# One decoder block on one core: channel-pair steps behind the weight splits at the passage to gate/up, and down's weight loads behind their splits

## The chip, the cores and the metric

The kernel runs on one core of one Trainium2 chip, as one launch. The metric is the device time of an execution in microseconds. The time before is the median of three runs. The profile is of one further execution, whose own time is given beside its span (first to last instruction).

## What is computed

One layer on 512 tokens of 2048 channels, in float32: an RMS norm, a joint input projection into three token mixers (dilated attention, convolution, sliding-window attention), an output projection with a residual, and a SwiGLU feed-forward part with 5632 hidden columns and a second residual. The change lies in the second half:

```python
def reference(x, ...):
    ...
        x = x + mix @ w_out[l]
        h2 = _rms_norm(x, norm2_g[l])
        x = x + (jax.nn.silu(h2 @ w_gate[l]) * (h2 @ w_up[l])) @ w_down[l]
    return x
```

## The kernel before

**Matrix products in three parts.** Every float32 product is made of three matmuls on rounded halves: high weight times high activation, low weight times high, high weight times low. A weight tile of 128 x 1024 is therefore split before use into `wh` (high) and `wl` (low). For gate/up and down a split is three operations: ScalarE (ACT) copies the raw weights, reordered, into `wn` in PSUM (L268) and into `wh` in SBUF (L269), and VectorE (DVE) subtracts to get `wl` (L270). There are three buffers of `wh` and `wl` and two of `wn`.

**Products of blocks.** Gate/up and down multiply 2 x 2 blocks with seven products in place of eight (Strassen's scheme in Winograd's form). Each of seven products needs a block or a sum of blocks of the weights and of the activations. The weight sums (`s`, `21`, `11`, made of the raw blocks `11`, `12`, `21`, `22`) are made by GpSimd (POOL) in place, at L172. `ORDER` and `D_ORDER` give the order of the products. Gate/up runs 11 blocks (`Up`) of 2 x 7 products of two units each, so 28 units of 12 matmuls per block (L1184, L1186, L1187); `u0`, `u1`, ... name the weights of half a block, `A` and `B` the two units of a product. Down runs 12 blocks of 14 units (`Down`, L1431 to L1433), with weights `d0` to `d11`; an A unit has 12 matmuls, a B unit 12 or 6.

**One list of weight units.** `works` holds every unit of the kernel in order: input projection, output projection, gate/up, down. Those of gate/up and down are marked `"moves"`. `next_unit()` hands out the next one, and beside that does three things ahead: `sums_now()` issues POOL's sums that are due at this unit, `split_up_to(u + SPLIT_AHEAD)` issues the splits up to two units ahead, and `pump(limit, most)` issues loads of raw weights (L242) on SyncE's (SP's) queue, as long as the next load's buffer is free and fewer than `limit` tiles are held, at most `most` of them. A buffer becomes free, in the program's order, when the last split that reads it is issued. Engines run their own instructions in the order in which the program issues them; SP's queue is one such order, with the loads of weights, of activations (`a<-od`, L1318), and the stores.

**Steps by ticks.** Work between projections is spread over the matmuls by a clock of its own, `Ticks`: `ticks.after(n, fn)` files a step, `ticks.tick()` runs what is due, `ticks.drain()` runs all. After each channel tile of the output projection is done, five steps follow at one tick each: `residual` (L984), `scale_x2` (store x2, scale it by the norm's weights, L992 and L994), `differences` (block differences of two channel tiles, L1014 to L1022; channel pair j is tiles j and j + 8), `high` (ACT casts, L1028) and `low` (DVE subtractions, L1034). Beside them the squares of x2 are added up into `ssum2` (L1004, and the addition that is recorded at L97). What `high` and `low` make, `ops[q, j]`, are gate/up's activations; pairs 0 to 3 are read by a block's first seven products, pairs 4 to 7 by the second seven. The projection ends with the tiles 6, 7, 14 and 15, that is with pairs 6 and 7.

**The passage.** Between the projection's last matmul and gate/up's first, the kernel before runs two ticks, issues the splits up to two units ahead, runs three more ticks and then drains all that is left.

**`norm2()`** turns `ssum2` into the norm's factor: eight small matmuls into `r2s` (L349), in one of the two PSUM buffers that `wn` uses, a DVE operation (L421) and a POOL operation (L422). It is called after gate/up's fourth unit. The factor is first used at the second seven products.

**Loads in down.** In `next_unit()` the units marked `"moves"` load before they split: at most two loads, and only into buffers that an earlier unit's split had freed. After the unit's matmuls, `load_next` issues one or two activation reads (two in the first block).

Of the kernel before, what the change touches and what calls it, by code (L numbers as in the profile page):

```python
# [52 lines left out]
RAW_BUFS = 8  # L53
RAW_EARLY = 5
SPLIT_BUFS = 3
X_AHEAD = 8
SPLIT_AHEAD = 2
# [59 lines left out]
def kernel(ctx: ExitStack, tc: tile.TileContext, xT, wi, wo, wgu, wd, cst_in, outT):  # L117
# [18 lines left out]
    ticks = Ticks()  # L136
# [12 lines left out]
    entries, works = [], []  # L149
# [4 lines left out]
    def take(buf, key, n=1024):  # L154
        assert buf not in held
        held[buf] = key
        raws[key] = (wp.tile([P, 1024], F32, name=f"w{key}", tag=f"raw{buf}", bufs=1), n)
        return raws[key][0]

    def drop(key):  # L160
        for buf in [b for b, k in held.items() if k == key]:
            held.pop(buf)
        return raws.pop(key)
# [5 lines left out]
    def plus(to, a, b, n, buf=None):  # L169
        def go():  # L170
            out = take(buf, to, n) if buf else raws[to][0]
            nc.gpsimd.tensor_add(out[:, :n], raws[a][0][:, :n], raws[b][0][:, :n])  # L172
        return go

    def up_block(pair, m, half, j):

        return [bass.AP(tensor=wgu.tensor, offset=wgu.offset + (4 * (pair + i * NP) + 2 * m + half) * P * 1024 + j * P,
                        ap=[[1024, P], [4 * P * 1024, 2], [1, 2 * P]]) for i in range(2)]
# [4 lines left out]
    for n in range(2 * NBLOCKS):  # L183
        base = len(works)
        keys = {c: {k: (k, f"u{n}{c}") for k in ("11", "12", "21", "22", "s")} for c in "AB"}
        for k in ("21", "11", "22", "12"):
            for i, c in enumerate("AB"):
                entries.append((bufs[c]["s" if k == "12" else k], keys[c][k],
                                up_block(n // 2 * 2, 2 - int(k[0]), int(k[1]) - 1, n % 2 * 4 + 2 * i)))
        for i, c in enumerate("AB"):  # L190
            key = keys[c]
            sums[base - 4 + i].append(plus(key["s"], key["21"], key["11"], 1024, bufs[c]["s"]))
            sums[base + i].append(plus(key["21"], key["21"], key["22"], 1024))
            sums[base + 2 + i].append(plus(key["11"], key["21"], key["11"], 1024))
            sums[base + 7 + i].append(plus(key["11"], key["11"], key["12"], 1024))
        works.extend((keys[c][k], last, "moves") for k, last in (
            ("s", True), ("11", False), ("22", True), ("11", False), ("21", True), ("12", True), ("11", True)) for c in "AB")
        bufs = {c: {"21": b["22"], "11": b["21"], "s": b["s"], "22": b["11"]} for c, b in bufs.items()}

    def down_block(g, i, half, first, end):  # L200
# [31 lines left out]
    at = {"entry": 0, "split": 0, "use": 0}  # L232

    def pump(limit, most=99):
        while at["entry"] < len(entries) and len(raws) < limit and entries[at["entry"]][0] not in held and most:
            most -= 1
            buf, key, parts = entries[at["entry"]]
            size = [part.shape[-1] * (part.shape[1] if len(part.shape) == 3 else 1) for part in parts]
            t, o = take(buf, key, sum(size)), 0
            for part, n in zip(parts, size):  # L240
                to = t[:, o:o + n]
                nc.sync.dma_start(to.rearrange("p (n f) -> p n f", n=part.shape[1]) if len(part.shape) == 3 else to, part)  # L242
                o += n
            at["entry"] += 1


    lows, late_lows = [], []

    def lows_now():
        while lows:  # L250
            fn, *args = lows.pop(0)
            fn(*args)  # L252
        if late_lows:
            pump(RAW_EARLY if at["use"] <= 20 else RAW_BUFS)

    def split_up_to(i):
        while at["split"] <= min(i, len(works) - 1):
            key, last, eng = works[at["split"]]
            t, n = drop(key) if last else raws[key]
            u = at["split"]  # L260
            hi = wp.tile([P, 1024], F32R, name=f"wh{u}", tag="hi", bufs=SPLIT_BUFS)
            lo = wp.tile([P, 1024], F32R, name=f"wl{u}", tag="lo", bufs=SPLIT_BUFS)
            if eng == "moves":

                near = psum["high"].tile([P, 1024], F32R, name=f"wn{u}", tag="h")
                src = t[:, :n].rearrange("p (n f c) -> p f n c", n=4, c=P)
                by = lambda x: x[:, :n].rearrange("p (f n c) -> p f n c", n=4, c=P)
                nc.scalar.copy(by(near), src)  # L268
                nc.scalar.copy(by(hi), src)  # L269
                nc.vector.tensor_sub(by(lo), src, by(near).bitcast(F32))  # L270
            elif eng or "high" not in psum:
                eng = eng or nc.vector

                (nc.vector.tensor_copy if u == 0 else nc.scalar.copy)(hi[:, :n], t[:, :n])  # L274
                lows.append((eng.tensor_sub, lo[:, :n], t[:, :n], hi[:, :n].bitcast(F32)))
                if not late_lows:
                    lows_now()
            else:
                near = psum["high"].tile([P, 1024], F32R, name=f"wn{u}", tag="h")
                nc.scalar.copy(near[:, :n], t[:, :n])  # L280
                nc.scalar.copy(hi[:, :n], t[:, :n])
                lows.append((nc.vector.tensor_sub, lo[:, :n], t[:, :n], near[:, :n].bitcast(F32)))
                if not late_lows:
                    lows_now()
            splits[u] = (hi, lo)
            at["split"] += 1

    def sums_now():
        for fn in sums.pop(at["use"], ()):
            fn()  # L290

    def next_unit():
        sums_now()
        u = at["use"]
        at["use"] += 1
        moves = works[u][2] == "moves"
        if moves:
            pump(RAW_BUFS, 2)
        lows_now()
        split_up_to(u + SPLIT_AHEAD)  # L300
        if not lows and not moves:
            pump(RAW_EARLY if u < 20 else RAW_BUFS)
        return splits.pop(u)

    def mm3(out, wh, wl, xh, xl, start, stop):
# [755 lines left out]
                m_hi.pop(row), m_lo.pop(row)  # L1061
    lows_now()

    ticks.tick()
    ticks.tick()
    split_up_to(at["use"] + SPLIT_AHEAD)
    for _ in range(3):
        ticks.tick()
    lows_now()
    ticks.drain()  # L1070
    b = m_hi = m_lo = r1b = mult_a = bias_a = bias_c = over = upper = None

    lows_now()
# [8 lines left out]
    def norm2():  # L1082

        b = psum["high"].tile([P, 1024], F32, name="r2s", tag="h")[:, :NT]
        n2["r"] = token_scale(ssum2, D, "n2", b)[1]
# [19 lines left out]
    def later(n, fn, *args, queue=evacs):  # L1105
        while len(queue) <= n:
            queue.append([])
        queue[n].append((fn, *args))
# [179 lines left out]
    def turn_x2(key):  # L1288

        z = turns[key] = slot("z")  # L1290
        for part in range(4):
            nc.sync.dma_start(by_blocks(z, part), turned(x2d, key, part))
# [14 lines left out]
    def load_next(n, limit=99):  # L1307
        while feed and n and len(acts) < limit:
            key = feed.pop(0)
            n -= 1  # L1310
            if len(key) == 4:
                y[key] = slot("y")
                nc.sync.dma_start(y[key], x2t[key])
            else:
                q, j = key
                acts[key] = slot(f"a{q}_{j}", F32R)
                at = LAID.index(q)
                nc.sync.dma_start(acts[key].bitcast(F32), od[j][:, at * T:(at + 1) * T])  # L1318

    for n in range(NBLOCKS):  # L1320
        blk = Up(n)
        for blk.first in (0, 4):
            for i, q in enumerate(ORDER):
                for c, _ in enumerate(blk.product(q)):
                    at_unit = (7 if blk.first else 0) * 2 + 2 * i + c
                    if n == 0 and at_unit == 3:
                        norm2()
                    if 1 <= n <= 8 and at_unit in (9, 23):
                        key = SUMS[2 * n - 2 + at_unit // 16]
                        turn_x2(key)  # L1330
                        later(6, turn_x2_now, key)
                    if n == NBLOCKS - 1 and blk.first:
                        load_next(2)
                if n == NBLOCKS - 1:
                    for j in range(4):
                        ops.pop((q, blk.first + j))
# [24 lines left out]
    class Down:  # L1361
# [74 lines left out]
        def sum(self, i, k, a):  # L1436
            return self.g, i, k, a
# [139 lines left out]
```

## Time and profile before

| what | value |
|---|---|
| median of three runs | 1874.36 us (1873.17 to 1876.38) |
| the profiled execution | 1873.66 us, span 1871.9 us |
| mean granted TensorE clock | 0.996 |
| PE (matmuls) busy | 1849.2 us, 99% of the span |
| DVE, ACT, POOL busy | 1432.8, 1321.8, 1106.1 us |
| moved by DMA | 330.36 MB, 176 GB/s over the span |

In the profile an engine's row tells when it worked and what ended its idle time. A line of the timeline has start and duration in microseconds, engine, source line, operation, the tile written and those read, the shapes, and in brackets the idle time before it with the instruction that ended it. In the view of windows each row is a stretch: its length, the busy time of PE, of the weight loads (PEld), DVE, ACT and POOL with their counts, the granted TensorE clock (1.00 is full speed), the busy share of the 16 DMA engines and their GB/s. SPq is SyncE's queue of DMA issues.

### The profile page before, as it was taken

To read this page: it belongs to the slowest core of one execution; us is meant where nothing else is said; L and a number is where in the kernel's file an instruction comes from. 1 tells how busy PE (TensorE), PEld (TensorE's weight loads), DVE (VectorE), ACT (ScalarE), POOL (GpSimd) and SP (SyncE) were. 2 spreads that over 40 slices of the span, in tenths; PEclk is the share of its full clock that TensorE was granted. 3 is DMA by queue.
4 is the path that set the end of the run, shared out by engine and by line. 5 is a ranking of instruction groups with operands and counts; after the bars stand their busy time and mean duration, and the time that the engine had idled before them with its cause. 6 is when DMAs were issued, how large, how long until landed. Compare 5 with 4: busy or idle time off the path is not lost.

```text
span 1871.9 us, 26621 instructions
## 1 busy us (share of the span) xinstructions
PE 1849.2 (99%) x8370; PEld 1530.4 (82%) x8370; DVE 1432.8 (77%) x2052; ACT 1321.8 (71%) x1794; POOL 1106.1 (59%) x850
## 2 busy tenths in 40 slices
PE   9999999999999999999999999999999899999998
PEld 7888888888887888888888888888888677888887
DVE  6778878998688777777777777777777577777777
ACT  6355644553457788887888888888888577778775
POOL 0135533100003467786887778868777789879775
PEclk9999999999999999999999999999999999999999
DMA  7242253343333356777867776777679887566545
GB/s 272 76 146 92 78 144 97 91 130 123 131 136 96 113 152 187 199 209 180 228 176 199 222 193 190 213 189 219 177 220 303 272 263 264 202 222 230 181 134 113
DMA packets 382988, 330.36 MB, mean 176 GB/s; under 512 B 171648, under 2 KB 311552, under 8 KB 382848
## 3 DMA queue, kind: packets, MB, share of 16 engines
q1 hardware_dynamic: 382704, 328.66, 59.3%
q8 instruction: 66, 1.08, 0.2%
q14 instruction: 74, 0.61, 0.1%
q10 hardware_dynamic: 144, 0.01, 0.0%
HBM read 255.56 MB, written 64.63 MB: 171 GB/s over the span
## 4 chain that ended last, share of the span: by engine, by line
PE 93%; POOL 2%; DMA 2%; issue 1%; DVE 1%; ACT 1%; SPq 0%; POOLq 0%; ACTq 0%; DVEq 0%
PE out L1184 15%; PE out L1186 15%; PE out L1187 15%; PE out L1431 6%; PE out L1432 6%; PE out L1433 6%; PE o L306 3%; PE o L308 3%; PE o L307 3%; PE cq L306 2%; PE cq L307 2%; PE cq L308 2%; PE ak L306 1%; PE aq L306 1%; PE av L306 1%
## 5 line engine op out<-in xcount | busy, mean ns | idle before, releaser
L1184 PE MATMUL out<-wh,h 128*128 128x512 f32 x1232 | 480.5, 390 | 4.3 <-ACT wh L269 4.3
L1186 PE MATMUL out<-wl,h 128*128 128x512 f32 x1232 | 480.4, 390 | 0.0
L1187 PE MATMUL out<-wh,h 128*128 128x512 f32 x1232 | 480.2, 390 | 0.0
L1184 PEld LDWEIGHTS out<-wh,h 128*128 128x128 f32 x1232 | 231.8, 188 | 52.8 <-ACT wh L269 4.7
L1186 PEld LDWEIGHTS out<-wl,h 128*128 128x128 f32 x1232 | 231.8, 188 | 48.4 <-DVE wl L270 0.3
L1187 PEld LDWEIGHTS out<-wh,h 128*128 128x128 f32 x1232 | 231.8, 188 | 48.3
L1431 PE MATMUL out<-wh,a 128*128 128x512 f32 x620 | 242.9, 392 | 11.5 <-ACT wh L269 11.5
L1432 PE MATMUL out<-wl,a 128*128 128x512 f32 x620 | 242.3, 391 | 0.8 <-DVE wl L270 0.8
L1433 PE MATMUL out<-wh,a 128*128 128x512 f32 x620 | 241.6, 390 | 0.0
L274 ACT CAST wh<-w 128x1024 fp32r<-128x1024 f32 (+2 forms) x94 | 96.8, 1031 | 152.6 <-PE o L307 64.5
L1431 PEld LDWEIGHTS out<-wh,a 128*128 128x128 f32 x620 | 117.2, 189 | 39.3 <-ACT wh L269 15.3
L252 DVE TENSOR_TENSOR wl<-w,wh 128x1024 fp32r<-128x1024 f32 (+2 forms) x95 | 113.5, 1195 | 41.3 <-ACT wh L274 39.9
L1432 PEld LDWEIGHTS out<-wl,a 128*128 128x128 f32 x620 | 117.2, 189 | 26.6 <-DVE wl L270 2.0
L1433 PEld LDWEIGHTS out<-wh,a 128*128 128x128 f32 x620 | 117.1, 189 | 23.6
L1441 DVE TENSOR_TENSOR y<-y,out 128x512 f32<-128x512 f32 x164 | 106.1, 683 | 21.9 <-PE out L1433 20.2
L517 DVE SCALAR_TENSOR_TENSOR y<-bu,cst,y 128x511 f32<-128x511 f32 (+14 forms) x120 | 89.8, 749 | 0.7
L306 PE MATMUL o<-mh_c,wh 128*128 128x512 f32 x128 | 51.1, 399 | 0.0
L306 PE MATMUL cq<-hh,wh 128*128 128x512 f32 x128 | 50.5, 395 | 0.0
L308 PE MATMUL o<-mh_c,wl 128*128 128x512 f32 x128 | 50.0, 391 | 0.0
L307 PE MATMUL cq<-hl,wh 128*128 128x512 f32 x128 | 49.9, 390 | 0.0
L307 PE MATMUL o<-ml_c,wh 128*128 128x512 f32 x128 | 49.9, 390 | 0.0
L308 PE MATMUL cq<-hh,wl 128*128 128x512 f32 x128 | 49.9, 390 | 0.0
(2376 smaller groups left out, 4881.3 us busy)
## 6 DMA issues: line engine op xcount, KB each, us to landing
od<-a SPq DMA_DIRECT2D x154, 256.0 KB, 4.1
a<-od SPq DMA_DIRECT2D x154, 256.0 KB, 5.6
w<-in_wi SPq DMA_DIRECT2D x58, 512.0 KB, 3.3
w<-in_wo SPq DMA_DIRECT2D x32, 512.0 KB, 3.3
x<-in_xT SPq DMA_DIRECT2D x16, 256.0 KB, 7.0
xr<-in_xT SPq DMA_DIRECT2D x16, 256.0 KB, 3.6
x2d<-xr SPq DMA_DIRECT2D x16, 256.0 KB, 2.0
z<-x2d SPq DMA_DIRECT2D x64, 64.0 KB, 3.8
```

Source lines behind the costliest of these rows:

```text
L252: fn(*args)
L274: (nc.vector.tensor_copy if u == 0 else nc.scalar.copy)(hi[:, :n], t[:, :n])
L306: nc.tensor.matmul(out, wh, xh, start=start, stop=False)
L307: nc.tensor.matmul(out, wh, xl, start=False, stop=False)
L308: nc.tensor.matmul(out, wl, xh, start=False, stop=stop)
L1184: nc.tensor.matmul(b, x[:, high], wh[:, s], start=c == f == 0 and q in (7, 1, 5, 2), stop=False, skip_group_check=True)
L1186: nc.tensor.matmul(b, x[:, high], wl[:, s], start=False, stop=False, skip_group_check=True)
L1187: nc.tensor.matmul(b, x[:, low], wh[:, s], start=False, stop=c == f == 1, skip_group_check=True)
L1431: nc.tensor.matmul(b[:, lo:hi], x[:, high], wh[:, s], start=start, stop=False, skip_group_check=True)
L1432: nc.tensor.matmul(b[:, lo:hi], x[:, high], wl[:, s], start=False, stop=False, skip_group_check=True)
L1433: nc.tensor.matmul(b[:, lo:hi], x[:, low], wh[:, s], start=False, stop=last, skip_group_check=True)
L1441: getattr(eng, op)(t, t, src)
```

## The change

Three edits.

1. At the passage, one split is issued, then one tick is run, then the next split; the ticks that were run there and the drain are gone. What is left of the steps of pairs 6 and 7 runs in gate/up's loop, one tick after each unit.
2. `norm2()` is called after gate/up's 13th unit in place of the 4th.
3. In `next_unit()` only gate/up's units (those before `turned_to`) load ahead of their split. Down's units load after it, again at most two, so that the load goes out one unit earlier in the program's order and into the buffer that this split has just freed, and in SP's queue it stands ahead of the activation reads of that unit.

```diff
             ("s", True), ("11", False), ("22", True), ("11", False), ("21", True), ("12", True), ("11", True)) for c in "AB")
+        turned_to = len(works)
...
         moves = works[u][2] == "moves"
-        if moves:
+        ahead = moves and u < turned_to
+        if ahead:
             pump(RAW_BUFS, 2)
         lows_now()
         split_up_to(u + SPLIT_AHEAD)
-        if not lows and not moves:
-            pump(RAW_EARLY if u < 20 else RAW_BUFS)
+        if not lows and not ahead:
+            pump(RAW_EARLY if u < 20 else RAW_BUFS, 2 if moves else 99)
         return splits.pop(u)
...
     lows_now()
 
-    ticks.tick()
+    split_up_to(at["use"] + SPLIT_AHEAD - 1)
     ticks.tick()
     split_up_to(at["use"] + SPLIT_AHEAD)
-    for _ in range(3):
-        ticks.tick()
-    lows_now()
-    ticks.drain()
     b = m_hi = m_lo = r1b = mult_a = bias_a = bias_c = over = upper = None
...
                     at_unit = (7 if blk.first else 0) * 2 + 2 * i + c
-                    if n == 0 and at_unit == 3:
+                    if ticks.due:
+                        ticks.tick()
+                    if n == 0 and at_unit == 12:
                         norm2()
```

The order in which the instructions are built changes at the passage on ACT and DVE, at `norm2` on PE, DVE and POOL, and from down's first block on in SP's queue. No instruction is added or removed.

## The prediction

> **What bounds the kernel now.** The page first: TensorE's row against the span.
>
> ```profile
> span 1871.9 us, 26621 instructions
> PE 1849.2 (99%) x8370; PEld 1530.4 (82%) x8370; DVE 1432.8 (77%) x2052; ACT 1321.8 (71%) x1794; POOL 1106.1 (59%) x850
> ```
>
> PE (TensorE's matmuls) is busy for 99% of the span, so an edit that removes no matmul can only win PE's idle time and the stretches in which its clock is low. The waits of PE say where it idles:
>
> ```profile
> PE out L1431 <- ACT wh L269: 11.5, 8, 2.6
> PE out L1184 <- ACT wh L269: 4.3, 1, 4.3
> PE out L1432 <- DVE wl L270: 0.8, 2, 0.7
> ```
>
> One wait of 4.3 us lies at L1184 (gate/up), eight of 11.5 us together at L1431 (down), both ended by ACT's `wh` at L269, a copy of a weight split; 0.8 us more by DVE's `wl`. The windows show the rest:
>
> ```profile
> 594.68:600.15 5.47, 5.47 (x12) 4.09 (x13) 3.61 (x4) 5.47 (x7) 2.39 (x1) 0.50 0.18 57
> 650.00:1400.00 750.00, 750.00 (x3310) 621.02 (x3310) 571.90 (x652) 625.20 (x760) 571.75 (x402) 1.00 0.72 196
> 1560.00:1860.00 300.00, 300.00 (x1325) 248.43 (x1324) 225.55 (x269) 229.12 (x259) 242.42 (x141) 1.00 0.60 190
> ```
>
> From 650 to 1400 us and from 1560 to 1860 us PE is busy without a gap at clock 1.00: nothing can be won there. Between 594.68 and 600.15 the granted clock is 0.50. So two places remain, the passage from output projection to gate/up and the first blocks of down, and the change edits both.
>
> I number gate/up's first units by their weights: 1 `s` A, 2 `s` B, 3 `11` A, 4 `11` B, 5 `22` A, 6 `22` B, 7 `11` A again. Each is 12 matmuls. PE's timeline in the passage:
>
> ```profile
> 582.08 0.39 PE L1184 MATMUL out<-wh,h 128*128 128x512 f32 x1
> 590.01 0.39 PE L1187 MATMUL out<-wh,h 128*128 128x512 f32 x1
> 594.68 0.79 PE L1184 MATMUL out<-wh,h 128*128 128x512 f32 x1 [4.28 <-ACT wh L269]
> 595.30 0.80 PE L1186 MATMUL out<-wl,h 128*128 128x512 f32 x1
> 600.15 0.95 PE L349 MATMUL r2s<-ones,ssum 128*128 128x1 f32 x8
> 600.96 0.48 PE L1184 MATMUL out<-wh,h 128*128 128x512 f32 x1
> ```
>
> **The passage, before.** From 582.08 (unit 1's first matmul) to 590.01 (unit 3's last) are 35 steps, so one takes 0.227 us and a unit 2.72 us. Without a wait unit 4 would start at 590.24 and unit 5 at 592.96. Unit 5 starts at 600.96: 8.0 us later. Of these 0.8 us (600.15 to 600.96) are the eight small `r2s` matmuls of `norm2`, which the change keeps and only moves. The loss that can be won is 7.2 us: 4.4 us until 594.68, and 2.7 us because twelve matmuls took 5.47 us at clock 0.50.
>
> **Why PE waited.** The splits of units 3 and 4 stand on ACT and DVE (VectorE) behind the steps of the last two channel pairs, pair 6 and pair 7 (L1020 to L1034 on DVE, L1028 on ACT), and one of those steps is held. DVE's timeline, and in the last row POOL's:
>
> ```profile
> 582.85 0.68 DVE L984 TENSOR_TENSOR xr<-xr,o 128x512 f32<-128x512 f32 x1
> 585.45 1.22 DVE L270 TENSOR_TENSOR wl<-w('11', 'u0A')_5517,wn 128x1024 fp32r<-128x1024 f32 x1 [1.32 <-ACT wn L268]
> 586.59 0.42 DVE L1034 TENSOR_TENSOR h<-ta,h 128x256 fp32r<-128x256 f32 x1
> 586.93 2.65 DVE L1034 TENSOR_TENSOR h<-tb,h 128x256 fp32r<-128x256 f32 x1
> 590.51 0.41 DVE L1020 TENSOR_TENSOR ta<-h,h 128x256 f32<-128x256 f32 x1
> 591.75 0.68 DVE L97 TENSOR_TENSOR ssum<-ssum,sr 128x512 f32<-128x512 f32 x1
> 592.36 0.42 DVE L1034 TENSOR_TENSOR h<-ta,h 128x256 fp32r<-128x256 f32 x1
> 594.03 1.21 DVE L270 TENSOR_TENSOR wl<-w('11', 'u0B')_5572,wn 128x1024 fp32r<-128x1024 f32 x1
> 586.90 2.39 POOL L172 TENSOR_TENSOR w('11', 'u0A')_5517<-w('21', 'u0A')_5464,w('11', 'u0A')_5517 128x1024 f32<-128x1024 f32 x1 [9.79 <-DVE wl L270]
> ```
>
> Unit 3's `wl` runs at 585.45 and unit 4's only at 594.03. Between them stand two sets of five subtractions. The first takes 0.34 us to the next (586.59 to 586.93), but the second lasts 2.65 us: POOL (GpSimd) starts its sum `11` + `21` at 586.90, freed by unit 3's `wl`, and the subtraction ends when POOL does. From the set's start to the next operation (590.51) are 3.92 us, 2.24 us over five such steps. [...]
>
> **The change, part 1: the order at the passage.** As the instructions are built, ACT now has: unit 3's split, pair 6's five casts, the last x2 scaling, unit 4's split, ..., unit 5's split, pair 7's casts, unit 6's split. DVE has: last `xr` addition, unit 3's `wl`, one `ssum` addition, unit 4's `wl`, pair 6's five subtractions, three operations L1020 to L1022, a copy from PSUM (L1197), unit 5's `wl`, the last `ssum` addition, unit 6's `wl`, pair 7's five subtractions. Nothing is added or removed, and SP's queue keeps its order here, so the loads cost nothing. ACT's steps come from its timeline before:
>
> ```profile
> 581.08 0.62 ACT L1004 ACTIVATE sr<-xr 128x512 f32<-128x512 f32 x1
> 582.56 0.41 ACT L1028 CAST h<-tb 128x256 fp32r<-128x256 f32 x1
> 583.79 0.72 ACT L994 ACTIVATE h<-xr,cst 128x512 f32<-128x512 f32 x1
> 584.42 1.00 ACT L268 CAST wn<-w('11', 'u0A')_5517 128x1024 fp32r<-128x1024 f32 x1
> 585.36 1.04 ACT L269 CAST wh<-w('11', 'u0A')_5517 128x1024 fp32r<-128x1024 f32 x1
> 586.30 0.63 ACT L1004 ACTIVATE sr<-xr 128x512 f32<-128x512 f32 x1
> ```
>
> Worked forward with the same durations. ACT's `sr` of 581.08 takes 0.62, so unit 3's `wn` starts at 581.7, its `wh` at 582.6 (0.94 each to the next, 584.42 to 585.36 to 586.30). Five casts at 0.31 (582.56 to 583.79 are four) run from 583.6 to 585.1, the scaling (0.63) to 585.7, then unit 4's `wn` to 586.7 and `wh` to 587.7. DVE: the `xr` addition of 582.85 needs 0.6 (as 591.75 to 592.36), unit 3's `wl` starts at 583.4 and frees POOL at 584.9, the `ssum` addition starts just before POOL, at 584.6. Unit 4's `wl` starts at 586.75, when `wn` is there, and ends by 588.0. Unit 4 needs it at 590.5: **the wait of 4.3 us is gone, and with it the low clock.**
>
> What is late next is unit 5's `wl`. POOL's sum of `11` B starts where unit 4's `wl` ends, so the lock falls on pair 6's set again: 587.9 plus 3.92 gives 591.8; L1020 to L1022 take 1.24 (590.51 to 591.75), the copy 0.6, so unit 5's `wl` runs 593.65 to 594.87. PE wants it for the second matmul of unit 5 at 593.19 and gets it at 594.93 (the lag 594.03 plus 1.21 to 595.30 shows 0.06): 1.74 us late, PE idle for 1.6. After that DVE recovers: unit 6's `wl` ends at 596.6 against 597.7 wanted. Pair 7's subtractions find POOL idle, since its next sum waits for unit 7's `wl`; that one ends at 600.0 against 600.5. So part 1 wins 7.2 - 1.74 = **5.5 us**. Bounds: 7.2 if the lock misses the set, 3.0 in the rival below. Pairs 6 and 7 are first read by PE a block half later, in units 16 and on, more than 25 us away: moving them costs nothing there.
>
> **Part 2: `norm2` at unit 13 instead of 4.** The eight `r2s` matmuls cost their 0.8 us later. DVE's reading of them waits for unit 13's end; behind it stands unit 16's `wl`, wanted 5.4 us (two units) later and needing 1.2: no cost. Behind POOL's tiny operation stand sums for units 21 on. Cost 0; if that cover failed, one `wl`, 1.2 us.
>
> **Part 3: down's loads.** Each unit's weight loads now stand in SP's queue behind the split that frees their buffer, one unit earlier in the order and ahead of one to three activation reads (`a<-od`). Two windows, then rows of the timelines of SP, POOL and PE:
>
> ```profile
> 1442.43:1479.64 37.21, 34.05 (x148) 26.97 (x147) 24.04 (x28) 24.23 (x27) 24.99 (x19) 1.00 0.98 310
> 1481.60:1484.23 2.63, 0.00 (x1) 0.01 (x1) 1.00 (x1) 2.05 (x3) 2.17 (x2) 0.99 1.06 389
> 1442.43 0.38 SPq L242 DMA_DIRECT2D w('12', 'd0A')_14032<-in_wd  x1
> 1475.11 0.38 SPq L242 DMA_DIRECT2D w('22', 'd1B')_14305<-in_wd  x1
> 1479.77 2.38 POOL L172 TENSOR_TENSOR w('21', 'd1A')_14068<-w('21', 'd1A')_14068,w('22', 'd1A')_14277 128x1024 f32<-128x1024 f32 x1 [6.28 <-DMA w('22', 'd1A')_14277<-in_wd]
> 1482.61 2.36 POOL L172 TENSOR_TENSOR w('21', 'd1B')_14163<-w('21', 'd1B')_14163,w('22', 'd1B')_14305 128x1024 f32<-128x1024 f32 x1 [0.46 <-DMA a<-od]
> 1496.58 0.50 PE L1431 MATMUL out<-wh,a 128*128 128x512 f32 x1 [1.77 <-ACT wh L269]
> ```
>
> SP sits until 1442.43, when POOL frees the buffer of `12` d0A; the change leaves that. From there until 1479.64 the DMA engines are 0.98 busy at 310 GB/s, 0.85 us for 256 KB: a transfer arrives by what is queued ahead of it. Counted in pieces of 256 KB from that load on, `11` d1A comes 20th, not 23rd; `11` d1B stays 29th; `22` d1A 40th, not 41st; `22` d1B 45th as before. POOL's sum at 1482.61 needs `22` d1B, and its chain leads to PE's start at 1496.58. From the next release (`12` d1B) on, `22` d2A stays 25th. So the first wait of down shrinks, the second takes its place, and the chain ends where it did: I take **0**. Bounds: the same stretch at the 389 GB/s of 1481.60 to 1484.23 would save 43 pieces times 0.17, 7.4 us; the other way two reads moved into the busy stretch cost 1.7.
>
> **Sum.** The profiled execution took 1873.66 us, 1.8 over its span; less 5.5 it is 1868.2. The median of the three runs is 0.7 above that execution, so I predict **1868.9 us**. A measurement of this kernel can tell about 0.2%, 3.75 us: faster means under 1870.6, slower over 1878.1.
>
> **Rivals.**
>
> *Down gains as well* (16%). The weights' earlier place lets POOL's chain start early: for it, 0.85 us for 256 KB is slow beside 0.67 at 389 GB/s; against it, the unchanged 45th place. With half of the bound, 3.7 us, **1865.2**.
>
> *The lock strikes twice* (13%). If the `ssum` addition is held by POOL's sum of `11` A, unit 4's `wl` starts 0.75 later (587.5), unit 5's wait is 2.5 us, and the clock falls again. Four windows on when it falls:
>
> ```profile
> 1494.80:1496.58 1.78, 0.01 (x2) 0.01 (x1) 1.00 (x1) 1.78 (x3) 1.78 (x3) 1.00 0.42 137
> 1497.84:1501.25 3.41, 3.41 (x9) 2.66 (x9) 3.41 (x5) 3.41 (x6) 3.41 (x4) 0.50 0.80 223
> 1530.02:1531.78 1.76, 0.01 (x2) 0.01 (x1) 0.99 (x1) 1.70 (x2) 1.76 (x2) 1.00 0.57 172
> 1531.78:1535.00 3.22, 3.22 (x14) 2.63 (x15) 1.42 (x3) 1.82 (x5) 3.22 (x5) 1.00 0.55 190
> ```
>
> An idle stretch of 1.78 us was followed by clock 0.50 for 3.4 us, one of 1.76 was not. So 2.3 idle would be, and costs 3.4 halved, 1.7: gain 7.2 - 2.5 - 1.7 = 3.0, **1871.4**. [...]
>
> *Down pays back* (8%). The reads that the weights pass push back each block's later pieces: 1.7 us in each of the three blocks d1 to d3 is 5.1, **1874.0**, no change. Against it stand the counts.
>
> *Slower* (6%). SP stops for POOL's sum with activation reads behind it, one unit longer than before. If these reads then come late, each of the eleven later blocks waits 2.7 us: plus 30, less 5.5, **1899**. It decides where a tile lands after its product. Against it: PE never waits for `a` in the waits above, only for `wh` and `wl`.
>
> The rest (2%) goes to no change. **Chances.** The forecast holds 55%, about a tenth of it beyond 1870.6. Faster 0.5 + 0.16 + 0.05 (the lighter cases of the second rival) = 0.71, slower 0.06, the same 0.05 + 0.08 + 0.08 + 0.02 = 0.23. The forecast's own range is 1867 to 1871; for 8 in 10 I add the first rival up to most of its bound and the second: 1862.5 to 1872.5.
>
> **What would show it.** Right: PE's wait at L1184 shrinks from 4.3 to 1 to 2 us, ends with DVE's `wl` (L1186) and no window there has clock 0.50; a pair-6 subtraction of 2.6 us stands right after unit 4's `wl`; down's waits stay near 12 us. Wrong: the clock falls in the passage, down's waits change by over 3 us, or PE waits for `a`.

## The result and the profile after

| what | before | after |
|---|---|---|
| median of the timed runs | 1873.59 us (8 runs, 1871.67 to 1876.38) | 1867.84 us (8 runs, 1866.97 to 1869.79) |
| ratio after / before | | 0.9971, 95% interval 0.9960 to 0.9982 |
| profiled execution's span | 1871.9 us | 1865.7 us |
| mean granted TensorE clock | 0.996 | 0.999 |

The changed kernel is 5.75 us faster (0.3%), where 5.5 were forecast. Its time is 1.1 us under the forecast 1868.9; 0.8 of that lies in the kernel before, whose median is 1873.59 us in these runs and was 1874.36 in the three. The first page lines of after, to set beside those of before:

```profile
span 1865.7 us, 26613 instructions
PE 1844.3 (99%) x8370; PEld 1527.3 (82%) x8370; DVE 1432.0 (77%) x2052; ACT 1321.4 (71%) x1794; POOL 1103.0 (59%) x850
```

PE's busy time fell by 4.9 us with the same 8370 matmuls. At clock 0.50 the twelve matmuls behind the wait counted as busy for 5.47 us in before, where a unit takes 2.72 us at 1.00, so busy time shrinks when low-clock stretches go. The waits of PE in after, each row with the total in us, the number of waits and the longest (line numbers have moved by up to three: `wh` is now L270, `wl` L271; in gate/up L1182 is the first of the three matmuls, and L1184 is now the one that reads `wl`):

```profile
PE out L1431 <- ACT wh L270: 11.6, 8, 2.7
PE out L1184 <- DVE wl L271: 1.6, 1, 1.6
PE out L1432 <- DVE wl L271: 1.6, 3, 0.7
```

The 4.3 us behind ACT's `wh` have become 1.6 us behind DVE's `wl`; the waits of down (L1431) are 11.6 us in 8, as before. PE's timeline at the passage in after, and two rows at the place where `norm2` now stands:

```profile
592.62 0.39 PE L1182 MATMUL out<-wh,h 128*128 128x512 f32 x1
594.62 0.50 PE L1184 MATMUL out<-wl,h 128*128 128x512 f32 x1 [1.61 <-DVE wl L271]
594.96 0.40 PE L1185 MATMUL out<-wh,h 128*128 128x512 f32 x1
...
619.00 0.95 PE L351 MATMUL r2s<-ones,ssum 128*128 128x1 f32 x8
619.81 0.49 PE L1182 MATMUL out<-wh,h 128*128 128x512 f32 x1
```

The eight `r2s` matmuls cost the 0.81 us at 619.00 that they cost at 600.15 before, and no wait follows them. The windows around the 1.61 us; the clock stays at 1.00 in both:

```profile
592.62:594.90 2.28, 0.67 (x3) 0.28 (x2) 2.28 (x4) 2.28 (x6) 0.00 (x0) 1.00 0.00 0
594.90:598.50 3.60, 3.60 (x17) 2.95 (x17) 3.60 (x9) 3.60 (x5) 0.00 (x0) 1.00 0.46 145
```

A stretch that holds the whole passage can be compared: from unit 1's start to the start of unit 15, behind both places of `norm2`. That is 628.29 - 582.08 = 46.21 us before (unit 15's first matmul starts at 628.29 there) and 622.68 - 581.74 = 40.94 us after, so **5.27 us are won in the passage**. Down's blocks d0 to d2, from their first matmul to that of d3, take 123.84 us before (1427.97 to 1551.81) and 123.43 after (1422.36 to 1545.79): 0.41 us less. DVE's and POOL's timelines in after show why 1.6 us are left:

```profile
586.47 1.22 DVE L271 TENSOR_TENSOR wl<-w('11', 'u0B')_5572,wn 128x1024 fp32r<-128x1024 f32 x1 [1.43 <-ACT wn L269]
587.61 0.42 DVE L1036 TENSOR_TENSOR h<-ta,h 128x256 fp32r<-128x256 f32 x1
587.95 2.63 DVE L1036 TENSOR_TENSOR h<-tb,h 128x256 fp32r<-128x256 f32 x1
590.50 0.41 DVE L1036 TENSOR_TENSOR h<-h,h 128x256 fp32r<-128x256 f32 x1
...
592.75 0.68 DVE L1195 COPY b0c<-out 128x512 f32<-128x512 f32 x1
593.35 1.21 DVE L271 TENSOR_TENSOR wl<-w('22', 'u0A')_5725,wn 128x1024 fp32r<-128x1024 f32 x1
...
584.68 2.64 POOL L172 TENSOR_TENSOR w('11', 'u0A')_5517<-w('21', 'u0A')_5464,w('11', 'u0A')_5517 128x1024 f32<-128x1024 f32 x1 [7.78 <-DVE wl L271]
587.86 2.43 POOL L172 TENSOR_TENSOR w('11', 'u0B')_5572<-w('21', 'u0B')_5467,w('11', 'u0B')_5572 128x1024 f32<-128x1024 f32 x1 [0.55 <-DVE wl L271]
```

Unit 4's `wl` frees POOL, POOL starts its sum at 587.86, and the second subtraction of pair 6, which starts at 587.95, lasts 2.63 us in place of 0.42; this is what the prediction and the expectation of e3 call the lock. DVE starts its operations from 582.63 to 597.55 in the order that the prediction lists, so everything behind this one comes that much later, unit 5's `wl` (593.35) last.

One correction to the words on the change: the first of the two split calls at the passage issues nothing, since the splits up to there are out already. What is built is one tick, then unit 3's split; unit 4's is issued by gate/up's second `next_unit`. The prediction worked from this built order. Every engine's count of work is the same in both kernels; the eight instructions by which the page's totals differ (26621 and 26613) only wait or issue.

### The profile page after: what moved, and what is told of

It is laid out like the page before. It is cut to its first block, busy times and chain, and to the rows that moved or that the text cites. A ratio compares the mean times of both kernels' runs of the same rounds, so it can differ in the third digit from the quotient of the medians.

```text
span 1865.7 us, 26613 instructions
## 1 busy us (share of the span) xinstructions
PE 1844.3 (99%) x8370; PEld 1527.3 (82%) x8370; DVE 1432.0 (77%) x2052; ACT 1321.4 (71%) x1794; POOL 1103.0 (59%) x850
## 4 chain that ended last, share of the span: by engine, by line
PE 92%; DMA 3%; POOL 2%; DVE 1%; issue 1%; ACT 1%; SPq 0%; POOLq 0%; DVEq 0%; ACTq 0%
PE out L1184 15%; PE out L1182 15%; PE out L1185 15%; PE out L1432 6%; PE out L1431 6%; PE out L1433 6%; PE o L310 3%; PE o L308 3%; PE o L309 3%; PE cq L308 2%; PE cq L309 2%; PE cq L310 2%; PE ak L308 1%; PE aq L308 1%; PE av L308 1%
## 5 line engine op out<-in xcount | busy, mean ns | idle before, releaser
L1184 PE MATMUL out<-wl,h 128*128 128x512 f32 x1232 | 479.4, 389 | 1.6 <-DVE wl L271 1.6
L1182 PE MATMUL out<-wh,h 128*128 128x512 f32 x1232 | 479.4, 389 | 0.0
L1184 PEld LDWEIGHTS out<-wl,h 128*128 128x128 f32 x1232 | 231.3, 188 | 50.0 <-DVE wl L271 2.0
L1182 PEld LDWEIGHTS out<-wh,h 128*128 128x128 f32 x1232 | 231.3, 188 | 47.8
L1431 PE MATMUL out<-wh,a 128*128 128x512 f32 x620 | 242.0, 390 | 11.6 <-ACT wh L270 11.6
L1431 PEld LDWEIGHTS out<-wh,a 128*128 128x128 f32 x620 | 116.8, 188 | 39.0 <-ACT wh L270 15.1
```

What stands on the lines that cost most here:

```text
L1182: nc.tensor.matmul(b, x[:, high], wh[:, s], start=c == f == 0 and q in (7, 1, 5, 2), stop=False, skip_group_check=True)
L1184: nc.tensor.matmul(b, x[:, high], wl[:, s], start=False, stop=False, skip_group_check=True)
L1431: nc.tensor.matmul(b[:, lo:hi], x[:, high], wh[:, s], start=start, stop=False, skip_group_check=True)
```

## Experiments

Each ran with runs of the kernel before on the same chip, and its ratio is against those (median of before: 1872.23 us beside each of e1 to e8, 1873.65 beside e9). Line numbers differ by a few from kernel to kernel.

**e1: the passage and `norm2` alone.** Down's loads stand where the kernel before has them.

```diff
-        turned_to = len(works)
...
-        ahead = moves and u < turned_to
-        if ahead:
+        if moves:
             pump(RAW_BUFS, 2)
...
-        if not lows and not ahead:
-            pump(RAW_EARLY if u < 20 else RAW_BUFS, 2 if moves else 99)
+        if not lows and not moves:
+            pump(RAW_EARLY if u < 20 else RAW_BUFS)
```

> The changed kernel's passage and its norm2 at unit 13, with down's weight loads left where the kernel before has them. My theory: the whole gain is made in the passage, so the time is 5.3 to 5.5 us below the kernel before, about 1868; PE's wait at L1184 is 1.6 us behind a wl, no window of the passage has clock 0.50, and down's waits are those of before (11.5 us in 8). Rival, that down's loads bring a part worth seeing: the gain stays at or under 4 us. Second rival, that the loads cost something: the gain is over 6.5 us.

Measured: 1867.21 us, ratio 0.9972 (0.9962 to 0.9983), so 5.0 us less. From unit 1 to unit 15 it takes 40.88 us (582.10 to 622.98), 5.33 less than before. Its waits:

```profile
PE out L1429 <- ACT wh L269: 11.9, 7, 2.6
PE out L1430 <- DVE wl L270: 2.0, 4, 0.7
PE out L1182 <- DVE wl L270: 1.5, 1, 1.5
```

The passage makes the whole gain; down's waits are as large as ever.

**e2: down's loads alone.**

```diff
-    split_up_to(at["use"] + SPLIT_AHEAD - 1)
+    ticks.tick()
     ticks.tick()
     split_up_to(at["use"] + SPLIT_AHEAD)
+    for _ in range(3):
+        ticks.tick()
+    lows_now()
+    ticks.drain()
...
-                    if ticks.due:
-                        ticks.tick()
-                    if n == 0 and at_unit == 12:
+                    if n == 0 and at_unit == 3:
                         norm2()
```

> Down's weight loads behind their splits alone; the passage and norm2 as in the kernel before. My theory: the waits of d1 change places and the chain ends where it did, so the time is within 1 us of the kernel before (0.4 less by the two traces); PE's 4.3 us at L1184 and the half clock behind it stay. Rival, down gains as well: 3 us or more less. Rival, down pays back: 1.5 us or more longer.

Measured: 1872.64 us, ratio 0.9996 (0.9988 to 1.0005): no difference that can be measured. The passage has its old wait again (4.6 us, and 0.57 as the mean clock of the next 5.4 us). How the waits in down's block d1 change places is seen in PE's timeline, first in before, then in e2:

```profile
1468.73 0.49 PE L1431 MATMUL out<-wh,a 128*128 128x512 f32 x1 [1.69 <-ACT wh L269]
1473.10 0.50 PE L1431 MATMUL out<-wh,a 128*128 128x512 f32 x1 [1.32 <-ACT wh L269]
1484.23 0.79 PE L1431 MATMUL out<-wh,a 128*128 128x512 f32 x1 [2.63 <-ACT wh L269]
1491.71 0.50 PE L1431 MATMUL out<-wh,a 128*128 128x512 f32 x1 [0.21 <-ACT wh L269]
```

```profile
1472.94 0.50 PE L1433 MATMUL out<-wh,a 128*128 128x512 f32 x1 [3.26 <-ACT wh L270]
1484.12 0.50 PE L1433 MATMUL out<-wh,a 128*128 128x512 f32 x1 [1.10 <-ACT wh L270]
1487.60 0.50 PE L1433 MATMUL out<-wh,a 128*128 128x512 f32 x1 [0.37 <-ACT wh L270]
1492.28 0.51 PE L1433 MATMUL out<-wh,a 128*128 128x512 f32 x1 [1.61 <-ACT wh L270]
1497.10 0.51 PE L1433 MATMUL out<-wh,a 128*128 128x512 f32 x1 [1.75 <-ACT wh L270]
```

With the row at 1496.58 that the prediction shows (1.77), before idles 7.6 us here and e2 8.1 us: the wait ahead of the first unit is gone, that ahead of the second has grown from 1.32 to 3.26, and both kernels come to the last unit of the stretch half a microsecond apart (1496.58 and 1497.10). Behind it the clock falls in before (the 3.4 us at 0.50 that the prediction shows, with matmuls of 0.63 us) and not in e2 (matmuls of 0.39 to 0.40 us from 1497.72 to 1499.33), which evens this out; earlier in the block both have one slow stretch, before at clock 0.50 from 1484.19 to 1487.60, and e2 with matmuls of 0.60 to 0.63 us from 1473.28 to 1476.24.

**e3: POOL's sum of `11` B held until pair 7's differences are done.** One tiny addition goes ahead of it on POOL (`held_by[j] = n4` is noted in `differences`).

```diff
+                if self.n == 0 and self.first == 0 and q == 1 and c == 1:
+                    nc.gpsimd.tensor_add(small("held", 1), held_by[7][:, :1], held_by[7][:, :1])
+                    held_by.clear()
```

> The changed kernel with one tiny addition on GpSimd (one column of pair 7's last difference) issued ahead of its sum of 11 B, so that this sum starts only after pair 7's operations at L1020 to L1024. Theory of the lock: no subtraction of pair 6 takes 2.6 us any more, each takes about 0.4; unit 5's wl comes about 2.2 us earlier, PE's wait of 1.6 us at L1184 is gone, and the time is about 1.6 us below the changed kernel, some 7 us below the kernel before. Rival, that DVE simply has too much in its queue ahead of that wl: the wait stays over 1 us and the time within 0.5 us of the changed kernel. Third possibility: the later sum delays its own readers, and a new wait appears from unit 9 on, where the trace would show a wh or wl of the sum of 11 B.

Measured: 1866.16 us, ratio 0.9968 (0.9955 to 0.9980). DVE's and POOL's timelines in e3:

```profile
587.85 0.42 DVE L1038 TENSOR_TENSOR h<-ta,h 128x256 fp32r<-128x256 f32 x1
588.18 0.42 DVE L1038 TENSOR_TENSOR h<-tb,h 128x256 fp32r<-128x256 f32 x1
588.52 0.42 DVE L1038 TENSOR_TENSOR h<-h,h 128x256 fp32r<-128x256 f32 x1
...
591.38 1.21 DVE L271 TENSOR_TENSOR wl<-w('22', 'u0A')_5725,wn 128x1024 fp32r<-128x1024 f32 x1
592.51 1.54 DVE L97 TENSOR_TENSOR ssum<-ssum,sr 128x512 f32<-128x512 f32 x1
...
590.94 0.19 POOL L1178 TENSOR_TENSOR held<-tb 128x1 f32<-128x1 f32 x1 [3.40 <-DVE tb L1025]
591.09 2.41 POOL L172 TENSOR_TENSOR w('11', 'u0B')_5572<-w('21', 'u0B')_5467,w('11', 'u0B')_5572 128x1024 f32<-128x1024 f32 x1
```

The long subtraction is gone with the sum moved out of its way, unit 5's `wl` comes 9.50 us after unit 1's start (591.38 - 581.88) in place of 11.61, and PE's wait at unit 5 has left the list. From unit 1 to unit 15 it takes 39.37 us (581.88 to 621.25), 1.57 less than after, so POOL's sum beside that subtraction is the cause of what was left. In the runs' times the step is under what they resolve (1.05 us between the medians of e1 and e3, taken on the same chip, with intervals that overlap); the trace carries this verdict. What is stretched now, beside POOL's sum of 591.09, is the `ssum` addition, 1.54 us in place of 0.69, and nothing that PE waits for is delayed by it. Unit 5's `wl` runs beside the same sum and is not stretched (1.21 us); one of its inputs, `wn`, lies in PSUM.

**e4: fewer activation reads ahead of block d1's weight loads.**

```diff
-                    load_next(2 if self.t == 0 else 1, FEED)
+                    load_next(2 if self.t == 0 and k < 3 else 1, FEED)
```

> The changed kernel with fewer activation reads ahead of block d1's weight loads: in the first block's last product groups one read is issued at a time instead of two. Theory of the queue (a transfer arrives by the number of 256-KB pieces ahead of it): the load of 22 d1B moves up by about 6 to 8 pieces of 0.85 us, its sum on GpSimd starts earlier by about as much until the chain of sums itself is the bound, and down's waits of 11.6 us at L1431 shrink by 3 to 5 us. Rival, that GpSimd's chain is the bound and not the arrival: the waits shrink by less than 1 us. Opposite sign: the reads that now come later keep PE waiting for a, and the kernel gets slower.

Measured: 1863.50 us, ratio 0.9952 (0.9939 to 0.9966), 8.7 us below before, where after was 5.75 below. In SP's order `22` d1B is now the 32nd transfer from the load of `12` d0A on, in place of the 37th (a weight tile counts once, where the prediction's count by 256 KB takes it twice; four reads of 64 KB count as one). POOL's timeline, in after and then in e4, at the sum that waits for it:

```profile
1477.89 2.40 POOL L172 TENSOR_TENSOR w('21', 'd1B')_14137<-w('21', 'd1B')_14137,w('22', 'd1B')_14285 128x1024 f32<-128x1024 f32 x1 [1.08 <-DMA w('22', 'd1B')_14285<-in_wd]
1482.58 2.40 POOL L172 TENSOR_TENSOR w('11', 'd1A')_14135<-w('21', 'd1A')_14042,w('11', 'd1A')_14135 128x1024 f32<-128x1024 f32 x1
1487.40 2.40 POOL L172 TENSOR_TENSOR w('11', 'd1B')_14171<-w('21', 'd1B')_14137,w('11', 'd1B')_14171 128x1024 f32<-128x1024 f32 x1
```

```profile
1473.06 2.40 POOL L172 TENSOR_TENSOR w('21', 'd1B')_14137<-w('21', 'd1B')_14137,w('22', 'd1B')_14275 128x1024 f32<-128x1024 f32 x1 [0.38 <-DMA a<-od]
1477.76 2.40 POOL L172 TENSOR_TENSOR w('11', 'd1A')_14135<-w('21', 'd1A')_14042,w('11', 'd1A')_14135 128x1024 f32<-128x1024 f32 x1
1482.61 2.41 POOL L172 TENSOR_TENSOR w('11', 'd1B')_14169<-w('21', 'd1B')_14137,w('11', 'd1B')_14169 128x1024 f32<-128x1024 f32 x1
```

(In e4 the profile names an activation read as what ended the wait of 0.38; the sum needs `22`.) Five transfers fewer at 0.85 us are 4.25 us; the sum starts 4.83 us earlier and all that hangs on it 4.8 us. PE's waits at L1431 shrink from 11.6 to 6.7 us, and blocks d0 to d2 take 118.82 us (1422.41 to 1541.23) in place of 123.43. The arrival is the bound, not POOL's chain, and the place in the queue sets the arrival. The size is less sure than the direction, since each trace is one execution: e3 and e5, whose loads and reads stand in the order of after, take 122.53 and 120.34 us for the same blocks. The runs carry the direction: the slowest of e4, 1864.67, is under the fastest of e1 and of e3 on the same chip (1865.72 and 1865.42).

**e5: unit 5's `wl` 1.2 us later.** Two additions whose results nobody uses, on DVE.

```diff
+                if self.n == 0 and self.first == 0 and q == 1 and c == 0:
+                    for i in range(2):
+                        nc.vector.tensor_add(slot(f"late{i}"), ssum2, ssum2)
                 wh, wl = next_unit()
```

> The changed kernel with two more additions of 512 columns on VectorE (about 1.2 us, their results unused) directly ahead of unit 5's wl. Both theories: PE's wait at L1184 grows from 1.6 to about 2.8 us. My reading of the clock in the traces (an idle stretch of 1.78 us and more was followed by 3.4 us at clock 0.50): the clock falls behind this wait as well, another 1.7 us, so the time is 2.9 us above the changed kernel. [...]

Measured: 1870.81 us, ratio 0.9988 (0.9979 to 0.9997); the ratio of after was 0.9971, so 0.0017, some 3.2 us, are lost at the median. The runs scatter from 1867.04 to 1874.58 and the intervals just overlap, so the trace decides. It is of the fastest run, whose blocks d0 to d2 take only 120.34 us; that hides the loss in its total. Windows at the wait:

```profile
592.70:595.50 2.80, 0.38 (x2) 0.00 (x0) 2.80 (x5) 2.80 (x7) 0.00 (x0) 0.95 0.00 0
595.50:597.00 1.50, 1.22 (x3) 1.03 (x4) 1.50 (x3) 1.50 (x4) 0.00 (x0) 0.50 0.03 9
597.00:598.50 1.50, 1.50 (x4) 1.12 (x4) 1.50 (x5) 1.50 (x2) 0.00 (x0) 0.50 0.55 178
```

PE idled for 2.7 us and the clock was 0.50 for the 3 us behind it; the passage takes 43.35 us (581.81 to 625.16), 2.4 more than in after, over twice the 1.09 us of added idle time. So the clock fell here behind an idle gap of 2.70 us.

**e7: e3 and e4 together** (both diffs above).

> The changed kernel with both edits that won alone: the tiny GpSimd addition ahead of the sum of 11 B, and one activation read at a time in the first block's last product groups. Theory that the two gains lie in different stages and add: 1.6 in the passage and 4.3 to 4.9 in down, so about 5.9 us below the changed kernel, near 1862 where the kernel before takes 1872.2 (11.5 to 12 us less). Rival, that they share a wait: the gain over the better of the two is under 0.7 us.

Measured: 1862.07 us, ratio 0.9941 (0.9928 to 0.9955), 10.2 us below before. The expectation's two figures did not agree: 1862 had been reckoned from the changed kernel's 1867.84, beside other runs of before, and was met; 11.5 to 12 us less was not. Against e4 (8.7 below) that is 1.4 us more, about e3's 1.57 in the passage; the passage itself takes 39.21 us. So the two gains add as far as the traces show: e7 keeps e3's gain in the passage, and its blocks d0 to d2 take 120.33 us (122.53 in e3, 118.82 in e4). By the runs alone e7 and e4 have overlapping intervals. What was too large is e4's part: 4.3 to 4.9 us by the waits, 3.0 over after by the runs.

**e8: e7, with one activation read at a time in the whole first block.**

```diff
-                    load_next(2 if self.t == 0 and k < 3 else 1, FEED)
+                    load_next(1, FEED)
```

> As the kernel with both edits, but one activation read at a time in all product groups of the first block. Theory of the queue: the loads of 11 d1A, 11 d1B and 22 d1A move up as well, the wait of 1.9 us at the end of block d1's first product shrinks, and the time falls by another 1 to 2 us. Rival, that activation reads become the late ones: PE waits for a, or the later blocks' weights come later, and the kernel gets slower than the one with both edits.

Measured: 1858.69 us, ratio 0.9932 (0.9920 to 0.9945), 13.5 us below before and, at the median, 3.4 below e7. Its waits:

```profile
PE out L1436 <- ACT wh L270: 4.3, 4, 1.8
PE out L1436 <- DMA a<-od: 2.0, 2, 1.5
PE out L1437 <- DVE wl L271: 1.9, 3, 0.8
```

Both theories are half right: the wait in block d1's first product is gone, and PE now waits 2.0 us for `a`, less than was won. Blocks d0 to d2 take 116.53 us, 3.8 less than in e7; the intervals of the two kernels' runs overlap.

**e9: e8 with down's loads back in their old places** (the diff of e1 on top of e8).

> As the kernel with one activation read at a time in the whole first block, but with down's weight loads back at the places that the kernel before gives them (the change's third part undone). In SP's order 22 d1B stays the 28th transfer after the load of 12 d0A and 22 d1A comes 26th instead of 25th; 11 d1A comes 15th instead of 12th and the activation reads around it two or three places earlier. Theory of the queue, that only the place of the last needed load sets the end: within 1 us of the kernel with the loads moved, so the change's part 3 is worth nothing here either; PE's two waits for a (2.0 us) shrink and a wait behind 11 d1A or 11 d1B of block d1 takes their place. Rival, that the change's part 3 is worth something once the reads no longer crowd the queue: 2 us or more slower.

Measured: 1860.16 us, ratio 0.9929 (0.9915 to 0.9942), 13.5 us below its own runs of before, as e8. Its waits:

```profile
PE out L1434 <- ACT wh L269: 7.5, 6, 1.7
PE out L1435 <- DVE wl L270: 1.9, 3, 0.8
```

The waits for `a` are gone and 3.2 us more behind `wh` stand in their place, though not where expected: they lie in block d1's later products, in d2 and ahead of d3 (1.42 us), and only 0.12 us at d1's second unit. By the runs, undoing the change's third part costs nothing here either; their intervals leave room for some 2.5 us, and in the two traces blocks d0 to d2 take 1.78 us longer in e9 (118.31 and 116.53), which is within the spread named under e4. So the rival's 2 us are not borne out and not excluded.

e8 and e9 are equal within their intervals, and both beat the kernel before and the changed kernel.

## Why the prediction was right

- **The wait of 4.3 us and the half clock go (7.2 us).** Right. The trace of after has neither, e1 wins the passage's gain without the third part, and e2 keeps both losses.
- **Unit 5's `wl` is late next, by 1.74 us.** Right, and close: it was to start 11.57 us after unit 1's first matmul (593.65 - 582.08) and starts 11.61 after it (593.35 - 581.74); PE idles 1.61 us for a forecast 1.6. What makes it late, POOL's sum beside pair 6's second subtraction (2.63 us in place of 0.42), is in the rows above, and e3 shows that it is the cause: with the sum held, the wait is gone.
- **The `ssum` addition slips in ahead of POOL.** Right, by 0.32 us: it starts at 584.36, POOL's sum at 584.68, and it takes its 0.69 us. So the lock does not strike twice. What was not foreseen is that POOL then pays: its sum takes 2.64 us instead of 2.39. Of the 256 sums of this size in after only two take over 2.47 us; the other (2.62 us, at 574.28) also starts while a VectorE subtraction of 0.41 us runs. In before no sum takes over 2.47 us. What makes these operations hold each other up no run shows; the runs show by how much each was stretched.
- **The sum of the passage, 5.5 us.** Measured 5.27 by the traces, 5.33 in e1. That the whole change measured 5.75 is closer than the terms deserve: the passage gave a little less than forecast and down 0.41 in place of 0, both under what the runs resolve.
- **`norm2` at no cost.** Right as far as it can be seen: 0.81 us for the eight matmuls at the new place and no wait behind them. It was not undone by itself, since `ssum2` is now complete only behind unit 5's `wl`; that the move costs or wins nothing rests on these rows.
- **Down's loads at 0.** The size is right (e2: 0.9996; traces 0.41 us less), and the argument by the place of `22` d1B in the queue is borne out by e4, where five places were worth 4.8 us. The wording of the step was only roughly right: the wait that takes the place of the first is the one ahead of the next unit (2.73 us in after, for 1.69 and 1.32 before), because `11` d1B kept its place, and the wait of 2.63 is split over three units (1.52, 0.42 and 1.62).
- **The rival of the second lock** fell for lack of its condition. Its price rested on the clock falling behind any idle gap of 1.78 us or more. That step was too simple: e5 bears the price out at 2.7 us, but in e1 a gap of 2.59 us was followed by clock 1.00 (last section), so what a gap of 2.3 us would have cost is not shown. The forecast did not hang on this: behind the 1.61 us left in the passage the clock was 1.00 in after.
- **Down gains as well** is false of the change, and true of down: by the number of reads ahead, not by the loads' place relative to their split, it gave 3 us in e4 and more in e8. The prediction had named the queue as what binds and had not asked who fills it.
- **Down pays back, and slower.** Neither came: blocks d0 to d2 are 0.41 us shorter, e2 shows no loss in the runs, and no wait of PE in after is ended by a read of `a`.

## What to carry to other kernels

Moving steps behind a late split wins what the split was late by, less what the moved steps then meet: look up which engine the earlier split sets free, and whether its next operation holds up what now stands there, as POOL's sum did with pair 6's subtraction (2.63 us in place of 0.42). For a load that arrives too late, count the transfers that stand ahead of it in the queue; here a new place for the load was worth nothing while this count stayed as it was (e2: ratio 0.9996), and thinning the reads ahead of it was worth about their number times their time (e4: five at 0.85 us, and a start 4.83 us earlier). When a bound is found in the profile, ask at once what else sets it than the edit at hand.

## What the runs showed of the hardware

**The clock behind idle gaps: their length alone did not decide it.** Between 560 and 1860 us the granted clock is 0.50 in before from 593.31 to 600.14, from 1484.19 to 1487.60 and from 1497.84 to 1501.26, and in after from 1468.27 to 1471.69; elsewhere in the two it is 1.00. It falls inside PE's gap of 4.28 us in before (until 594.68), at the end of that of 2.63 us (until 1484.23), 1.26 us behind that of 1.77 us (until 1496.58), and 1.01 us behind that of 2.73 us in after (until 1467.26). The gaps of 1.75, 1.69, 1.43 and 1.32 us in before and of 1.72, 1.62, 1.61, 1.52, 1.44 and 1.42 in after have clock 1.00 behind them. Two longer gaps, of nearly the same length, part ways in e1. In each row the idle time is the length less PE's busy time:

```profile
1462.03:1465.44 3.41, 0.83 (x4) 0.41 (x3) 1.22 (x1) 1.99 (x2) 1.47 (x2) 1.00 1.11 341
1465.44:1468.86 3.42, 3.42 (x10) 2.65 (x9) 0.60 (x1) 1.65 (x2) 3.42 (x3) 0.50 1.15 260
1475.68:1479.10 3.42, 2.09 (x10) 1.39 (x8) 0.00 (x0) 0.78 (x1) 2.71 (x2) 1.00 1.07 378
1479.10:1482.51 3.41, 2.15 (x9) 1.75 (x10) 1.51 (x2) 3.16 (x6) 3.33 (x3) 1.00 0.74 272
1482.51:1485.92 3.41, 3.41 (x17) 2.59 (x15) 0.93 (x1) 1.69 (x4) 3.33 (x4) 1.00 0.03 7
```

The 2.58 us of the first row are followed by a row at clock 0.50. The gap of 2.59 us that ends at 1480.36 lies with 1.33 us in the third row and with 1.26 in the fourth, and the clock is 1.00 in the last three rows. What sets the clock was not tested. Nor do the runs show whether the same gap is followed by the same clock in every execution, since each kernel left one trace.

**POOL's sums and VectorE's operations stretched each other, but not `wl`.** A VectorE addition of 0.69 us started in after 0.32 us ahead of POOL's sum, and this sum took 2.64 us, 0.25 more than in before; POOL's sum stretched VectorE operations from 0.42 to 2.63 us (after) and from 0.69 to 1.54 us (e3), but not `wl` (1.21 us in e3, 1.22 at 586.47 in after). `wl` reads one input from PSUM; whether that is why it was spared was not tested.
